# The order of seven products in a two-layer encoder: another tree of sums and bank copies

## Chip, cores and metric

The kernel runs on one core of one Trainium2 chip. The metric is the device time of one execution in microseconds. Before the change three runs gave 909.03, 909.10 and 910.12 us, median 909.1.

## What is computed

The reference is a trunk of two layers on 256 tokens of width 1024, all in float32:

```python
for l in range(DEPTH):   # 2
    x = x + 0.5 * swiglu(rms_norm(x, ffn1_norm[l]), ffn1_w_gate[l], ffn1_w_up[l], ffn1_w_down[l])
    h = rms_norm(x, mix_norm[l])
    ...   # windowed attention and differential attention on h @ w_in[l]
    x = x + jnp.concatenate([out_a, out_b], axis=-1) @ w_out[l]
    x = x + 0.5 * swiglu(rms_norm(x, ffn2_norm[l]), ffn2_w_gate[l], ffn2_w_up[l], ffn2_w_down[l])
return rms_norm(x, final_norm)

def swiglu(h, w_gate, w_up, w_down):
    return (jax.nn.silu(h @ w_gate) * (h @ w_up)) @ w_down
```

The hidden width of an FFN is 2816. The change lies in its products with w_gate and w_up.

## The kernel before

**Products.** A float32 product is made of three matmuls in fp32r: each operand is split into a high part and the rest (low), and high x high, low x high and high x low are added in PSUM. Weights come in blocks of four 128-row chunks by 512 columns (1 MB). SP loads a block into one of six buffers, tile name `raw`. `emit_split` then splits it in two halves: ScalarE casts a half to its high part (`CAST w<-raw`), VectorE subtracts for the low part (`TENSOR_TENSOR w<-raw,w`). A block is multiplied with the 256 tokens; one that meets 128 tokens takes 12 matmuls, one that meets all takes 24.

**Groups by seven.** An FFN's hidden columns are worked in five groups of 512 (0 to 4) and a rest. In 15 groups (2, 3, 4 in the first FFN, 1 to 4 in the other three) gate and up together are a 2 by 2 product: tokens in two halves t, the depth of 1024 in two halves, gate and up as the two columns. The eight products of 12 matmuls are replaced by seven on sums, as in Strassen's scheme. The weight blocks are a (gate, upper depth), b (up, upper), c (up, lower), d (gate, lower). The sums of blocks are made in place: b into a, and c into b, by accumulate DMAs that POOL issues (`gather`; rows `POOL ... DMA raw<-in_ffn_w_up_dram`); c and then d into a by VectorE (`plus`; rows `raw<-raw,raw`). A buffer holds a, then ab, then abc, then abcd, and each is split into w before the next is added. The sums of tokens are made once per FFN by `make_sums` (tiles `q` and `v`).

**Around them.** A group of `by_sevens` also takes two blocks of w_down: dn1 (second column half of the group before last) and dn0 (first half of the group before), 24 matmuls each. dn0 multiplies the hidden block of the group before, which must be transposed first (`turn_one`: four transposes for each of two token halves, a copy `CAST s<-ps` or `s<-xy` to the high part by ScalarE and a subtract by VectorE). The products of a group are summed in PSUM banks `ps` and `xy` with copies by ScalarE. VectorE adds the last sums, ScalarE applies silu, and `up` multiplies into the hidden block (two operations `s<-tmp,hr,tmp`).

**The order.** Every engine works its instructions in the order in which the program issues them (`Kept`). `specs` lists the blocks in the order in which TensorE takes them. `ahead(n)` issues loads, additions and splits for block halves up to number n; where it is called within a group, and how far, stands in the tables `LEAD` (`first` for group 1, `mid`, `last`; other names for the FFN's start and end). A step's `prep` (an addition or an accumulate DMA) is issued once the splits of the step before are.

Of the kernel before, what the change touches and what calls it, by code (L numbers as in the profile page):

```python
# [14 lines left out]
P = 128  # L15
# [15 lines left out]
SEVEN = ((2, 3, 4), (1, 2, 3, 4))  # L31
LEAD = dict(start=(2, 7, 8, 6),
            open0=(2, 0, 0, 2, 3, 6, 8, 6, 5, 6, 1, 10, 1, 5, 7, 6, 8, 0),
            first=(1, 1, 2, 8, 12, 15, 16, 19, 19, 22, 22),
            mid=(2, 8, 12, 12, 15, 15, 20, 20, 20, 22, 23),
            last=(1, 7, 12, 14, 15, 15, 17, 20, 20, 21, 22),
            mid0=(4, 9, 12, 15, 15, 15, 19, 19, 19, 22, 24),
            last0=(2, 8, 12, 13, 15, 15, 19, 20, 20, 22, 25),
            first0=(0, 0, 3, 6, 6, 11, 11, 11, 12, 18, 18),
            open=(10, 11, 9, 7, 11, 11, 9, 5),  # L40
            close0=(6, 3, 7, 5, 6, 10, 3, 10, 5, 11, 4, 6, 1),
            close=(0, 8, 9, 9, 6, 2, 7, 6, 1, 10, 5, 4, 8),
# [4 lines left out]
def trunk(ctx: ExitStack, tc: tile.TileContext, x, n1, g1, u1, d1, nm, w_in, sink,  # L47
# [59 lines left out]
    class Step:  # L107
        def __init__(self, kn, n, moves, key=None, prep=None, src=None, free=None, behind=None, early=0):
            self.kn, self.n, self.moves, self.prep, self.early = kn, n, moves, prep, early
            self.behind, self.added = behind, behind is not None or moves is None  # L110
# [20 lines left out]
    def seven(wg, wu, c0, below, down):  # L131

# [44 lines left out]


# [69 lines left out]
    def ahead(n):  # L248

        n = min(n, 2 * len(specs) - 1)  # L250
        while True:
# [10 lines left out]
            elif at["dma"] < min(at["use"] + AHEAD, len(specs)) and (specs[at["dma"]].moves is None or len(raws) < N_RAW):  # L262
                if specs[at["dma"]].moves is not None:
                    for _ in emit_dma(at["dma"]):
                        pass
                at["dma"] += 1
            else:
                break
# [19 lines left out]
    for l in range(DEPTH):  # L288
        def ffn_specs(wg, wu, wd, sevens):
# [4 lines left out]
            for g in range(1, NGRP):  # L294
                downs = [down(g - 1, h) for h in range(2)]
                if g in sevens:
                    specs.extend(seven(wg[l], wu[l], g * 512, down(g - 2, 1) if g > 1 else None, downs[0]))
# [12 lines left out]
            for n in range(4 if 1 in sevens else 9):  # L310
                specs[base + n].lead = "open" + "0" * (1 not in sevens), n
            for n in range(6):
                specs[n - 6].lead = "close" + "0" * (1 not in sevens), n

        ffn_specs(g1, u1, d1, SEVEN[l > 0])
# [23 lines left out]
        ffn_specs(g2, u2, d2, SEVEN[1])  # L339
# [4 lines left out]
    class Norm:  # L344
# [14 lines left out]
        def turn(self, j, of=range(2), sl=None):  # L359
            sl = halves(bank()) if sl is None else sl  # L360
            for i in of:
                for t in range(2):
                    pe.transpose(sl[:, i, t * P:(t + 1) * P], xk[:, t, (2 * j + i) * P:(2 * j + i + 1) * P], ident)
# [25 lines left out]
        def make_sums(self):  # L389
# [3 lines left out]
            (t0, t1), (b0, b1) = [(t[:, :, 0:P], t[:, :, P:S]) for t in self.xg]  # L393
# [27 lines left out]
            high(s2)  # L421
            yield
            low(2, b0_)
            low(3, s2)
# [262 lines left out]
    def ffn(norm, aside=None, before=None, final=False, sevens=SEVEN[1]):  # L687
# [21 lines left out]
        def prod(xo, w, acc=None):  # L709

            first = acc is None
            if first:
                acc = bank()
# [29 lines left out]
        stage = 0 if before is take_x else 1  # L743

        def by_sevens(h, groups, old):


            flat = lambda: tmp().rearrange("p a n -> p (a n)")
            xy = pair()
            take = lambda: weights(99, True)  # L750
            for g in groups:
                start, late = old is None, g == groups[-1]
                first = 2 * at["use"] - (2 if start else 0)
                caps = iter(LEAD[("first" if start else "last" if late else "mid") + "0" * (stage == 0)])

                def go():
                    ahead(first + next(caps))

                go()
                p1 = prod(norm.quarter(0, 0), take())  # L760
                act.activation(xy[0], p1, AF.Copy, scale=-1.0)
                if start:
                    act.activation(xy[1], p1, AF.Copy, scale=-1.0)
                    new = [turn_one(h, 0)]
                    go()
                    new.append(turn_one(h, 1))
                    go()
                else:
                    below(old, g - 2, 1, take())
                    go()  # L770
                    new = [turn_one(h, 0), turn_one(h, 1, xy[1])]
                    go()
                prod(norm.summed(0), take(), xy[0])
                if not start:
                    act.activation(xy[1], p1, AF.Copy, scale=-1.0)
                go()
                if start:
                    prod(norm.quarter(0, 1), take(), p1)
                below(by_token(new), g - 1, 0, take())
                go()  # L780
                if not start:
                    prod(norm.quarter(0, 1), take(), p1)
                g0 = silu(flat(), p1, 0)
                go()
                old = by_token(new)
                p5 = prod(norm.summed(1), take())
                act.copy(p1, p5)
                go()
                prod(norm.summed(2), take(), xy[1])
                go()  # L790
                prod(norm.summed(3), take(), p5)
                e = flat()
                act.copy(e, p5)
                u1, u0 = flat(), flat()
# [495 lines left out]
```

## Time and profile before

| from the profiled execution | |
| --- | --- |
| median of three runs | 909.1 us |
| span of the profiled execution | 907.5 us |
| TensorE (PE) busy | 899.1 us, 99% |
| VectorE (DVE) busy | 785.9 us, 87% |
| ScalarE (ACT) busy | 609.8 us, 67% |
| GpSimd (POOL) busy | 63.2 us, 7% |
| DMA | 200.83 MB, mean 221 GB/s |

PE is busy in nearly all of the span, and PEld, the weight loads beside the matmuls, in 83% of it. The matmuls are pipelined and their ends modelled, so the starts of the next rows tell more than durations. All busy times are sums over stretches with different limits; the groups by seven are the largest part (twelve of 30.8 us and three first ones of 25.4).

### The profile page before, as it was taken

What the parts mean: (1) busy time and instruction counts of PE and PEld (TensorE: products, weight loads), DVE (VectorE), ACT (ScalarE), POOL (GpSimd) and SP (SyncE); (2) the same over time, 40 slices, a digit from 0 to 9 for tenths busy, and PEclk for the clock granted to TensorE, in tenths of its full rate; (3) what the DMA queues carried; (4) which work ended last, traced back from release to release, by engine and by line L of the source; (5) the groups of instructions that cost most, each with busy time, mean ns of one, the idle gap of its engine ahead of it and who ended that gap; (6) DMA issues with size and microseconds to landing.
All of it is one profiled execution on the core that took longest, in us unless ns stands there. A gap on an engine that the chain in (4) does not pass through costs nothing.

```text
span 907.5 us, 12030 instructions
## 1 busy us (share of the span) xinstructions
PE 899.1 (99%) x4468; PEld 751.0 (83%) x4468; DVE 785.9 (87%) x1069; ACT 609.8 (67%) x970; POOL 63.2 (7%) x79
## 2 busy tenths in 40 slices
PE   9999999999999999999999999999999999999997
PEld 7888888888888888888888888888888888888886
DVE  5968999879987899999778999988888978999894
ACT  6946677666776776677575776667667785776660
POOL 0401000000001001000000001000000000101011
PEclk9999999999999999999999999999999999999999
DMA  9998897954148798897976898899611786898731
GB/s 328 355 287 213 236 309 247 268 143 179 47 150 241 174 265 247 247 300 256 279 204 171 250 278 258 252 303 248 182 57 48 263 223 166 234 312 255 219 114 47
DMA packets 114331, 200.83 MB, mean 221 GB/s; under 512 B 3678, under 2 KB 31648, under 8 KB 114272
## 3 DMA queue, kind: packets, MB, share of 16 engines
q1 hardware_dynamic: 97616, 167.66, 54.4%
q0 software_dynamic: 16096, 31.75, 20.1%
q8 instruction: 35, 0.57, 0.2%
q10 hardware_dynamic: 560, 0.66, 0.2%
q14 instruction: 24, 0.20, 0.1%
HBM read 199.00 MB, written 1.05 MB: 220 GB/s over the span
## 4 chain that ended last, share of the span: by engine, by line
PE 98%; DMA 1%; issue 0%; SPq 0%; DVE 0%; POOLq 0%; POOL 0%
PE ps L62 73%; PE xy L62 25%; DMA xk<-in_x_dram 1%; SPq L172 0%; DVE s L62 0%; DVE xk L62 0%; POOLq L1285 0%; POOL rf L62 0%; SPq L469 0%; SPq L465 0%; DVE tot L62 0%; DVE tmp L62 0%
## 5 line engine op out<-in xcount | busy, mean ns | idle before, releaser
L62 DVE TENSOR_TENSOR w<-raw,w 128x1024 fp32r<-128x1024 f32 (+1 forms) x458 | 476.4, 1097 | 34.6 <-ACT w L62 33.2
L62 PE MATMUL ps<-w,s 128*128 128x512 f32 (+1 forms) x2046 | 473.6, 389 | 0.0
L62 PEld LDWEIGHTS ps<-w,s 128*128 128x128 f32 x2046 | 379.9, 188 | 78.7 <-issue 0.8
L62 ACT CAST w<-raw 128x1024 fp32r<-128x1024 f32 (+1 forms) x457 | 403.9, 954 | 54.0 <-DVE raw L62 38.7
L62 PE MATMUL xy<-w,s 128*128 128x512 f32 x528 | 125.8, 392 | 0.0
L62 PEld LDWEIGHTS xy<-w,s 128*128 128x128 f32 x528 | 98.2, 188 | 20.4
L62 PE MATMUL xy<-w,q 128*128 128x512 f32 x360 | 88.1, 393 | 0.0
L62 PEld LDWEIGHTS xy<-w,q 128*128 128x128 f32 x360 | 66.5, 188 | 13.3
L62 PE MATMUL ps<-s,w 128*128 128x512 f32 (+1 forms) x384 | 69.8, 338 | 0.0
L62 DVE TENSOR_TENSOR raw<-raw,raw 128x2048 f32<-128x2048 f32 x30 | 68.6, 2288 | 0.5
L62 POOL DMA_DIRECT2D raw<-in_ffn_w_up_dram x30 | 38.9, 1313 | 430.1 <-DVE w L62 264.9
L62 PEld LDWEIGHTS ps<-s,w 128*128 128x128 f32 x384 | 58.6, 188 | 8.5
L62 ACT ACTIVATE s<-ps,gcol 128x256 fp32r<-128x256 f32 (+1 forms) x80 | 31.4, 479 | 34.0 <-PE ps L62 34.0
L62 ACT CAST s<-ps 128x512 fp32r<-128x512 f32 x36 | 20.4, 592 | 43.2 <-PE ps L62 43.0
L62 PE MATMUL ps<-w,q 128*128 128x512 f32 x180 | 43.2, 389 | 0.0
L62 PE MATMUL ps<-w,v 128*128 128x512 f32 x180 | 43.2, 389 | 0.0
L62 DVE TENSOR_TENSOR s<-ps,s 128x512 fp32r<-128x512 f32 x36 | 24.1, 686 | 19.5 <-ACT s L62 19.3
L62 PEld LDWEIGHTS ps<-w,v 128*128 128x128 f32 x180 | 33.8, 188 | 7.0
L62 PEld LDWEIGHTS ps<-w,q 128*128 128x128 f32 x180 | 33.8, 188 | 7.0
L62 ACT ACTIVATE s<-s,negm 128x256 f32<-128x256 f32 x64 | 31.8, 498 | 5.3 <-DVE negm L62 5.3
L62 ACT COPY ps<-ps 128x512 f32<-128x512 f32 x15 | 8.6, 570 | 34.4 <-PE ps L62 34.4
L62 DVE SCALAR_TENSOR_TENSOR s<-ps,gcol,s 128x256 fp32r<-128x256 f32 x48 | 20.3, 477 | 13.0 <-ACT s L62 12.9
(131 smaller groups left out, 584.3 us busy)
## 6 DMA issues: line engine op xcount, KB each, us to landing
raw<-in_ffn_w_down_dram SPq DMA_DIRECT2D x44, 1024.0 KB, 7.0
raw<-in_ffn_w_gate_dram SPq DMA_DIRECT2D x39, 1024.0 KB, 7.7
raw<-in_ffn_w_up_dram SPq DMA_DIRECT2D x39, 1024.0 KB, 7.1
raw<-in_ffn_w_up_dram POOLq DMA_DIRECT2D x30, 1024.0 KB, 10.0
raw<-in_w_in_dram SPq DMA_DIRECT2D x14, 1024.0 KB, 6.7
raw<-in_ffn_w_gate_dram SPq DMA_DIRECT2D x8, 512.0 KB, 7.9
raw<-in_ffn_w_up_dram SPq DMA_DIRECT2D x8, 512.0 KB, 8.9
raw<-in_w_in_dram SPq DMA_DIRECT2D x8, 512.0 KB, 6.0
```

Of the source, the lines that this page charges most:

```text
L62: ins = issue(*a, **k)
```

## The change

The seven products are formed by another scheme of sums. In a group TensorE took a, dn1, the transposes, bc, dn0, d, ab, c, abc, abcd (in group 1: a, the transposes, bc, d, dn0, ...). It now takes a, dn1, the transposes, d, dn0, abc, ab, bc, c, abcd (in group 1: a, the transposes, d, dn0, ...). ScalarE made two copies with a factor of -1 (`ACTIVATE xy<-ps`) and two plain ones in a group; now it makes four plain ones (a's bank to Q, abc's to Y, ab's to SBUF, bc's to Q). VectorE added twice and subtracted once from the last product; now it adds twice, and silu of the second half reads the bank itself. The sign goes into `up` by a second scale, minus half of r. `make_sums` makes its four sums in another order. c is loaded beside the step ab; the accumulate DMA to a is issued before the one to b; the tables of how far the splits run ahead are new and stand apart for each FFN. The transposes of the norm have one start and one stop per tile.

```diff
@@ -29,17 +29,28 @@
 N_RAW, N_S4 = 6, 28
 IN_FFN, IN_MIX = 8, 6
 SEVEN = ((2, 3, 4), (1, 2, 3, 4))
+ORDER = (("a", "d", "dn0", "ab", "abc", "bc", "c", "abcd"),
+         ("a", "dn1", "d", "dn0", "ab", "abc", "bc", "c", "abcd"))
...
-            first=(1, 1, 2, 8, 12, 15, 16, 19, 19, 22, 22),
-            mid=(2, 8, 12, 12, 15, 15, 20, 20, 20, 22, 23),
+            next1=(10, 10, 14, 14, 14, 17, 19, 19, 20, 24),
+            more1=(7, 8, 8, 9, 9, 14, 18, 18, 19, 19, 20),
+            last1=(3, 7, 7, 9, 14, 14, 14, 17, 20, 20, 23),
+            open1=(1, 6, 7, 3, 4, 11, 5, 9),
...
-    def seven(wg, wu, c0, below, down):
-
-
-
+    def seven(wg, wu, c0, order):
 
         a, b, c, d = [object() for _ in range(4)]
         w = {a: rows(wg, c0, 512, 0, 4), b: rows(wu, c0, 512, 0, 4), c: rows(wu, c0, 512, 4, 4), d: rows(wg, c0, 512, 4, 4)}
@@ -149,17 +158,23 @@
                 dve.tensor_tensor(raws[to], raws[to], raws[x], op=ALU.add)
             return prep
 
-        steps = [Step(4, 512, load(b), key=b, behind=gather(c, b)), down, Step(4, 512, load(d), key=d, free=[])]
-        if below is not None:
-            steps.insert(0, below)
-        else:
-            steps.insert(1, steps.pop())
-        steps[0].prep = lambda: issue(gather(b, a), 1)
-        return [Step(4, 512, load(a), key=a, free=[])] + steps + [
-                Step(4, 512, None, src=a, free=[]),
-                Step(4, 512, load(c), key=c, free=[]),
-                Step(4, 512, None, prep=plus(c, a), src=a, free=[c], early=1),
-                Step(4, 512, None, prep=plus(d, a), src=a, free=[a, d])]
+        parts = dict(a=Step(4, 512, load(a), key=a, free=[]),
+                     d=Step(4, 512, load(d), key=d, free=[]),
+                     ab=Step(4, 512, None, src=a, free=[], also=(c, w[c])),
+                     abc=Step(4, 512, None, prep=plus(c, a), src=a, free=[]),
+                     bc=Step(4, 512, load(b), key=b, added=True),
+                     c=Step(4, 512, None, src=c, added=False),
+                     abcd=Step(4, 512, None, prep=plus(d, a), src=a, free=[a, d], early=2))
+        steps = [parts[o] if isinstance(o, str) else o for o in order]
+        def begin():
+            if b in raws:
+                issue(gather(c, b), 1)
+            else:
+                parts["bc"].behind = gather(c, b)
+
+        steps[steps.index(parts["a"]) + 1].prep = lambda: issue(gather(b, a), 1)
+        steps[steps.index(parts["d"]) + 1].prep = begin
+        return steps
...
+    def load_also(s):
+        key, src = s.also
+        raws[key] = raw = wp.tile([P, 4, 512], F32, tag="raw", bufs=N_RAW, name=nm_("raw"))
+        sp.dma_start(raw, src)
...
-            def add(x, y, op):
+            def add(x, y):
                 v = tmp().rearrange("p a (c s) -> p (a c) s", c=2)
-                dve.tensor_tensor(v, x, y, op=op)
+                dve.tensor_tensor(v, x, y, op=ALU.subtract)
+                return v
+
+            def less(x, y):
+                v = tmp().rearrange("p a (c s) -> p (a c) s", c=2)
+                dve.scalar_tensor_tensor(v, in0=x, scalar=-1.0, in1=y, op0=ALU.mult, op1=ALU.subtract)
...
-            v = add(t1, t0, ALU.subtract)
-            s1 = add(t1, b1, ALU.subtract)
-            yield
-            high(v)
+            (t0, t1), (b0, b1) = [(t[:, :, 0:P], t[:, :, P:S]) for t in self.xg]
+            s1 = add(b1, t1)
             high(s1)
             yield
-            low(0, v)
-            s2 = add(t0, s1, ALU.subtract)
-            low(1, s1)
-            b0_ = add(b0, s2, ALU.subtract)
-            yield
-            high(b0_)
+            s2 = less(s1, t0)
+            low(0, s1)
             high(s2)
             yield
-            low(2, b0_)
-            low(3, s2)
+            low(1, s2)
+            yield
+            v = add(t0, t1)
+            high(v)
+            yield
+            b0_ = less(s2, b0)
+            low(2, v)
+            high(b0_)
+            yield
+            low(3, b0_)
...
+            self.nhr = tmp("nhr", 2, (P, 2))
+            dve.tensor_scalar_mul(self.nhr, self.r, -0.5)
...
-        def up(h, acc, g, t):
+        def up(h, acc, g, t, by=None):
             n = acc.shape[1]
-            dve.scalar_tensor_tensor(h[:, t, :n], in0=acc, scalar=norm.hr[:, t:t + 1], in1=g, op0=ALU.mult, op1=ALU.mult)
+            by = norm.hr if by is None else by
+            dve.scalar_tensor_tensor(h[:, t, :n], in0=acc, scalar=by[:, t:t + 1], in1=g, op0=ALU.mult, op1=ALU.mult)
...
-        stage = 0 if before is take_x else 1
-
-        def by_sevens(h, groups, old):
-
-
-            flat = lambda: tmp().rearrange("p a n -> p (a n)")
-            xy = pair()
-            take = lambda: weights(99, True)
+        flat = lambda: tmp().rearrange("p a n -> p (a n)")
+
+        def taker(order):
+            left, have = iter(order), {}
+
+            def take(name):
+                while name not in have:
+                    have[next(left)] = weights(99, True)
+                return have.pop(name)
+            return take
+
+        def by_seven(banks, take, go, then):
+
+            A, B, Q, Y = banks
+            prod(norm.quarter(0, 0), take("a"), A, True)
+            act.copy(Q, A)
+            then("a")
+            prod(norm.quarter(0, 1), take("d"), Q)
+            g0 = silu(flat(), Q, 0)
+            go()
+            then("d")
+            prod(norm.summed(1), take("abc"), A)
+            act.copy(Y, A)
+            go()
+            prod(norm.summed(0), take("ab"), B, True)
+            e = flat()
+            act.copy(e, B)
+            go()
+            then("abc")
+            prod(norm.summed(2), take("bc"), A)
+            act.copy(Q, A)
+            u1 = flat()
+            dve.tensor_tensor(u1, A, e, op=ALU.add)
+            go()
+            then("bc")
+            prod(norm.summed(3), take("c"), Y)
+            u0 = flat()
+            dve.tensor_tensor(u0, Y, e, op=ALU.add)
+            h = blk(F32)
+            up(h, u0, g0, 0, norm.nhr)
+            go()
+            prod(norm.quarter(1, 1), take("abcd"), Q)
+            g1 = silu(flat(), Q, 1)
+            go()
+            up(h, u1, g1, 1, norm.nhr)
+            return h
+
+        def by_sevens(h, groups, old, sums):
+
+            A, Q = bank(), bank()
+            B, Y = pair()
+            banks = (A, B, Q, Y) if old is None else (A, Q, B, Y)
+            upto, more = [0], [None]
+
+            def go(table=None):
+                if table is not None:
+                    upto[0] = 2 * at["use"] - (2 if table == "next" else 0)
+                    more[0] = iter(LEAD[table + str(which)])
+                ahead(upto[0] + next(more[0]))
+
             for g in groups:
...
+                go("next" if g == 1 else "last" if g == groups[-1] else "more")
+                new = []
+                take = taker(ORDER[g > 1])
+
+                def then(what):
+                    if what == "a":
+                        if g > 1:
+                            below(old, g - 2, 1, take("dn1"))
+                            go()
+                        for t in range(2):
+                            new.append(turn_one(h, t, banks[1 + 2 * t]))
+                            go()
+                            next(sums, None)
+                    elif what == "d":
+                        below(by_token(new), g - 1, 0, take("dn0"))
+                        for _ in sums:
+                            pass
+                        go()
+
+                h = by_seven(banks, take, go, then)
                 old = by_token(new)
...
+            below(old, groups[-1] - 1, 1, weights(look[0] - 3))
...
```

In the order of the engines, in the second FFN (layer 0), where group 1 begins, ScalarE before: `raw_508` is the buffer of b with c, `raw_509` that of d, `raw_518` that of dn0; `raw_495` is a's. The ACTIVATE rows from `ps_528` are silu, those to `xy` the two copies of product a, the s4 rows the transposed hidden block.

```order
L62 CAST q_562_2925<-tmp_546_2893 128x4x128
L62 CAST q_563_2927<-tmp_547_2895 128x4x128
L62 ACT_TABLE_LOAD
L62 ACTIVATE tmp_567_2961<-ps_528_2793,r_545_2890 128x512
L62 ACTIVATE tmp_568_2963<-ps_529_2794,r_545_2890 128x512
L62 CAST q_569_2965<-tmp_565_2933 128x4x128
L62 CAST v_570_2967<-tmp_564_2930 128x4x128
L62 ACTIVATE xy_572_2998<-ps_575_3003 128x512
L62 ACTIVATE xy_573_2999<-ps_575_3003 128x512
L62 CAST s4_577_3023<-ps_576_3018 128x512
L62 CAST s4_579_3031<-ps_578_3026 128x512
L62 CAST w_582_3084<-raw_495_2610 128x1024
```

Now, with `raw_489` the buffer of a:

```order
L73 CAST w_555_2929<-raw_489_2602 128x1024
L73 CAST w_557_2933<-raw_489_2602 128x1024
L73 ACT_TABLE_LOAD
L73 ACTIVATE tmp_560_2952<-ps_522_2784,r_539_2881 128x512
L73 ACTIVATE tmp_561_2954<-ps_523_2785,r_539_2881 128x512
L73 CAST w_567_2987<-raw_489_2602 128x1024
L73 COPY ps_564_2984<-ps_563_2983 128x512
L73 CAST s4_569_3008<-xy_565_2985 128x512
L73 CAST q_571_3013<-tmp_570_3011 128x4x128
L73 CAST s4_572_3019<-xy_566_2986 128x512
L73 CAST w_573_3022<-raw_489_2602 128x1024
```

The two casts of ab and the first of abc moved from behind the transposed block to ahead of silu, and of the copy to Q. On VectorE at that place, before:

```order
L62 TENSOR_TENSOR w_558_2916<-raw_518_2719,w_557_2915 128x1024
L62 TENSOR_TENSOR w_560_2920<-raw_518_2719,w_559_2919 128x1024
L62 TENSOR_TENSOR q_562_2925<-tmp_546_2893,q_562_2925 128x4x128
L62 TENSOR_TENSOR tmp_564_2930<-s4_542_2865,tmp_547_2895 128x512
L62 TENSOR_TENSOR q_563_2927<-tmp_547_2895,q_563_2927 128x4x128
L62 TENSOR_TENSOR tmp_565_2933<-s4_543_2882,tmp_564_2930 128x512
L62 SCALAR_TENSOR_TENSOR s4_571_2993<-xy_530_2795,hr_548_2897,tmp_567_2961 128x512
L62 SCALAR_TENSOR_TENSOR s4_571_2993<-xy_531_2796,hr_548_2897,tmp_568_2963 128x512
```

And now:

```order
L73 TENSOR_TENSOR w_554_2926<-raw_503_2668,w_553_2925 128x1024
L73 TENSOR_TENSOR w_556_2930<-raw_489_2602,w_555_2929 128x1024
L73 TENSOR_TENSOR w_558_2934<-raw_489_2602,w_557_2933 128x1024
L73 TENSOR_TENSOR raw_489_2602<-raw_489_2602,raw_512_2710 128x2048
L73 SCALAR_TENSOR_TENSOR s4_562_2980<-xy_524_2786,hr_542_2888,tmp_560_2952 128x512
L73 SCALAR_TENSOR_TENSOR s4_562_2980<-xy_525_2787,hr_542_2888,tmp_561_2954 128x512
L73 TENSOR_TENSOR w_568_2988<-raw_489_2602,w_567_2987 128x1024
```

The subtracts of ab and the addition of c moved to ahead of the two operations that make the hidden block (`s4<-xy,hr,tmp`).

The third group of the same FFN, ScalarE around the copies of the transposed block (`s4_686`, `s4_687`), before; `raw_618` is a's buffer:

```order
L62 CAST w_680_3515<-raw_649_3354 128x1024
L62 CAST w_682_3519<-raw_662_3405 128x1024
L62 CAST s4_686_3531<-ps_685_3526 128x512
L62 CAST s4_687_3538<-xy_573_2999 128x512
L62 CAST w_688_3541<-raw_662_3405 128x1024
L62 CAST w_690_3545<-raw_618_3207 128x1024
L62 CAST w_692_3549<-raw_618_3207 128x1024
L62 CAST w_694_3553<-raw_663_3407 128x1024
L62 ACTIVATE xy_573_2999<-ps_677_3473 128x512
```

Now, with `raw_615` as a's buffer and `s4_673`, `s4_674` as the transposed block:

```order
L73 COPY ps_564_2984<-ps_563_2983 128x512
L73 CAST w_671_3505<-raw_615_3207 128x1024
L73 CAST s4_673_3513<-xy_565_2985 128x512
L73 CAST s4_674_3520<-xy_566_2986 128x512
L73 CAST w_675_3523<-raw_615_3207 128x1024
L73 ACTIVATE tmp_677_3540<-ps_564_2984,r_539_2881 128x512
L73 CAST w_678_3566<-raw_615_3207 128x1024
L73 CAST w_680_3570<-raw_615_3207 128x1024
L73 CAST w_682_3574<-raw_649_3372 128x1024
```

The casts of ab stood behind the transposed block; the first now stands ahead of it, and the casts of abc stand just behind, where d's, ab's and c's did.

VectorE at the end of the group ahead of that one, before: the two subtracts of the next a (`raw_618`), then from the last product's neighbours the sums (`tmp`) and the hidden block (`s4_667`):

```order
L62 TENSOR_TENSOR w_657_3393<-raw_618_3207,w_656_3392 128x1024
L62 TENSOR_TENSOR w_659_3397<-raw_618_3207,w_658_3396 128x1024
L62 TENSOR_TENSOR w_661_3402<-raw_630_3267,w_660_3401 128x1024
L62 TENSOR_TENSOR tmp_666_3436<-xy_573_2999,tmp_664_3433 128x512
L62 TENSOR_TENSOR tmp_665_3435<-xy_572_2998,tmp_664_3433 128x512
L62 SCALAR_TENSOR_TENSOR s4_667_3439<-tmp_666_3436,hr_548_2897,tmp_650_3368 128x512
L62 TENSOR_TENSOR tmp_668_3453<-ps_619_3211,tmp_665_3435 128x512
```

And now, with `raw_615` as the next a:

```order
L73 TENSOR_TENSOR w_646_3365<-raw_615_3207,w_645_3364 128x1024
L73 TENSOR_TENSOR tmp_651_3401<-ps_563_2983,tmp_650_3386 128x512
L73 TENSOR_TENSOR w_653_3404<-raw_615_3207,w_652_3403 128x1024
L73 TENSOR_TENSOR tmp_654_3420<-xy_566_2986,tmp_650_3386 128x512
L73 SCALAR_TENSOR_TENSOR s4_655_3422<-tmp_654_3420,nhr_543_2890,tmp_627_3290 128x512
```

The second subtract of a, after which a's accumulate DMA may start, moved to behind the first sum, which waits for product bc.

More of the change, by code (lines that the diff above doesn't have):

```diff
@@ L362, in turn @@
                 for t in range(2):
-                    pe.transpose(sl[:, i, t * P:(t + 1) * P], xk[:, t, (2 * j + i) * P:(2 * j + i + 1) * P], ident)
+                    pe.matmul(sl[:, i, t * P:(t + 1) * P], lhsT=xk[:, t, (2 * j + i) * P:(2 * j + i + 1) * P], rhs=ident,
+                              is_transpose=True, start=i == of[0] and t == 0, stop=i == of[-1] and t == 1)
             return sl
@@ L741, in below @@
             tokens(accs[h], of, w, 4 * g, last=(FC - 1, G4 - 1) if final and h else FC - 1, order=order)
-        stage = 0 if before is take_x else 1
-        def by_sevens(h, groups, old):
-            flat = lambda: tmp().rearrange("p a n -> p (a n)")
-            xy = pair()
-            take = lambda: weights(99, True)
-            for g in groups:
[L752 to L784, printed above, removed]
-                old = by_token(new)
[L786 to L794, printed above, removed]
-                dve.tensor_tensor(u0, xy[1], e, op=ALU.add)
-                dve.tensor_tensor(u1, xy[0], e, op=ALU.add)
-                h = blk(F32)
-                up(h, u0, g0, 0)
-                go()
-                p4 = prod(norm.quarter(1, 1), take(), p1)
-                g1 = flat()
-                dve.tensor_tensor(g1, p4, u1, op=ALU.subtract)
-                go()
-                silu(g1, g1, 1)
-                up(h, u1, g1, 1)
-                go()
-            w = weights(look[0] - 3)
-            below(old, groups[-1] - 1, 1, w)
@@ L870, in ffn @@
             g = gate(gs)
-            next(sums)
         else:
@@ L902, in ffn @@
                 if hh == 0:
-                    next(sums, None)
+                    for _ in sums:
+                        pass
         gu = pair()
@@ L950, in ffn_close @@
         tail(1)
-        ahead(2 * at["use"] + LEAD["close"][-1])
+        ahead(2 * at["use"] + LEAD[f"close{which}"][-1])
         group(1, [(1, t) for t in range(2)])
```

67 lines of the change are left out of this document (37 added, 30 removed).

## Prediction

> **What bounds the kernel now.** I read the page's first part, then the chain.
>
> ```profile
> PE 899.1 (99%) x4468; PEld 751.0 (83%) x4468; DVE 785.9 (87%) x1069; ACT 609.8 (67%) x970; POOL 63.2 (7%) x79
> PE 98%; DMA 1%; issue 0%; SPq 0%; DVE 0%; POOLq 0%; POOL 0%
> ```
>
> TensorE is busy for 899.1 of 907.5 us and carries 98% of the chain: nothing that another engine saves is worth time by itself, since TensorE never waits for it. The profiled span of 907.5 us stands 1.6 us below the median of 909.1 us; I add stalls to the span and then those 1.6 us. About 0.2% (1.8 us) is what a measurement of this kernel can tell from no change.
>
> Then the stretches, one per group of the second FFN (328.01, 358.83) and the third (534.41); columns are PE, PEld, DVE, ACT, POOL, clock, DMA share, GB/s.
>
> ```profile
> 328.01:358.83 30.82, 30.82 (x142) 25.61 (x141) 29.46 (x27) 21.98 (x27) 2.48 (x2) 1.00 0.88 240
> 534.41:565.22 30.81, 30.81 (x141) 25.61 (x141) 29.50 (x28) 21.85 (x27) 2.54 (x3) 1.00 0.92 263
> ```
>
> TensorE fills the whole period at full clock, but VectorE has only 1.3 us to spare and the DMA rings are at 0.9. So the question is whether a reordered group still delivers each operand before TensorE asks. Who asks when, from the PE timeline of one group (start, duration, operation):
>
> ```profile
> 531.75 11.05 PE L62 MATMUL ps<-w,s 128*128 128x512 f32 x48
> 542.64 0.60 PE L62 MATMUL ps<-ident,s 128*128 128x128 f32 x4
> 543.43 2.98 PE L62 MATMUL xy<-w,q 128*128 128x512 f32 x12
> ```
>
> 48 matmuls take 10.89 us, so a product of 12 takes 2.72 and the eight transposes with their switch 0.8 to 0.9. A changed group, from its first matmul: a 0, dn1 2.7, transposes 8.2, d 9.0, dn0 11.8, abc 17.2, ab 19.9, bc 22.6, c 25.4, abcd 28.1, end 30.8.
>
> **The price of the work itself.** Durations by form:
>
> ```profile
> L62 DVE TENSOR_TENSOR w<-raw,w 128x1024 fp32r<-128x1024 f32 x354 | 411.7, 1219 | 30.5 <-ACT w L62 29.3
> L62 ACT CAST w<-raw 128x1024 fp32r<-128x1024 f32 x354 | 348.1, 1051 | 50.9 <-DVE raw L62 38.7 <-DMA raw<-in_ffn_w_up_dram 11.8
> L62 DVE TENSOR_TENSOR raw<-raw,raw 128x2048 f32<-128x2048 f32 x30 | 68.6, 2288 | 0.5
> L62 DVE SCALAR_TENSOR_TENSOR s<-tmp,hr,tmp 128x512 f32<-128x512 f32 x30 | 22.3, 742 | 0.0
> L62 DVE TENSOR_TENSOR tmp<-ps,tmp 128x512 f32<-128x512 f32 x15 | 10.3, 685 | 0.3
> L62 ACT ACTIVATE xy<-ps 128x512 f32<-128x512 f32 x30 | 17.2, 581 | 10.5 <-PE ps L62 10.5
> L62 ACT COPY tmp<-ps 128x512 f32<-128x512 f32 x15 | 8.7, 582 | 5.0 <-PE ps L62 5.0
> L62 ACT COPY ps<-ps 128x512 f32<-128x512 f32 x15 | 8.6, 570 | 34.4 <-PE ps L62 34.4
> L62 ACT CAST s<-ps 128x512 fp32r<-128x512 f32 x36 | 20.4, 592 | 43.2 <-PE ps L62 43.0
> L62 DVE TENSOR_TENSOR s<-ps,s 128x512 fp32r<-128x512 f32 x36 | 24.1, 686 | 19.5 <-ACT s L62 19.3
> ```
>
> The third VectorE operation of a group (685 ns, 15 of them) goes: 10.3 us of VectorE, worth 0, because TensorE covers it. ScalarE still makes four copies per group; 30 negating ones (581) become plain (570 to 582): 0. Four small operations for the second half-scale and eight sums as scalar-tensor-tensor (742 against about 685): 4 x 0.17 + 8 x 0.06 = 1.2 us of VectorE, under TensorE's products outside the groups: 0. TensorE issues the same matmuls: 0. The transposes of the norm with one start and stop per tile: same shapes, 0. The copies that TensorE now needs back: Q after a has the eight transposes as cover in the first group (0.8 against 0.57) and dn1 besides later; Y after abc has ab and bc, 5.4; Q after bc has c, 2.7; with 0.6 each they fit unless ScalarE is held. On the queues: SP loads the same blocks, c with ab rather than ahead of bc; on POOL a's accumulate DMA now precedes b's, and b's waits for its load some 3 us after a's issue, 27 us ahead of the next a's, so it holds nothing. The sum consists only of stalls that the order makes.
>
> **Stall one: the first group of the FFNs two to four.** There a's accumulate DMA and its neighbours run so in the second FFN (POOL's issue, its time to landing from the DMA view of that window, then TensorE and ScalarE):
>
> ```profile
> 290.14 1.31 POOL L62 DMA_DIRECT2D raw<-in_ffn_w_up_dram  x1
> raw<-in_ffn_w_up_dram POOLq DMA_DIRECT2D x1, 1024.0 KB, 8.6
> 298.62 1.28 ACT L62 ACT_TABLE_LOAD   x1
> 302.63 2.88 PE L62 MATMUL ps<-w,s 128*128 128x512 f32 x12
> 305.36 1.04 PE L62 MATMUL ps<-ident,s 128*128 128x128 f32 x8
> 307.48 2.98 ACT L62 CAST w<-raw 128x1024 fp32r<-128x1024 f32 x3
> ```
>
> Before, a+b lands at 298.75 and is first touched at 307.48. Now both casts of a+b, their subtracts and the addition of c stand ahead of the two operations that make the hidden block, which the transposes want at 305.36. The sum: 298.75, two casts (2 x 1.05) to 300.85, second subtract 1.2 to 302.1, addition 2.29 to 304.4, two scalings of 0.7 to 305.1 and 305.8. The second half of the transposes wants it at 305.8, and the cast of abc (waiting for the addition) stands ahead of the copy of Q: 304.4 + 1.05 + 0.57 = 306.0, wanted at 306.2. Slack zero: I take 0.3 each for hand-overs, three times 0.9 us; ends 0 and, with a landing 2 us later, 6.
>
> **Stall two: the later groups.** The tables put a's second half behind the two additions to it, and behind bc's copy. VectorE's subtracts follow each other at 1.15 to 1.2. The hidden block's lows are done 10.6 us into the group (transposes to 9.0, second cast 0.6 to 9.7 at the earliest, its low 0.7, 0.2 of hand-overs); from there the second half of ab 1.15, addition 2.3 and its cast's wait 1.1, abc 2.3, bc 2.3, c 1.15, addition 2.3, c 1.15, abcd 2.3, a 1.15, u1 0.65, a 1.15 = 29.8. So a's accumulate DMA issues 1.0 us ahead of its group, where before it was 1.2 ahead. What differs is who waits: the cast of ab now stands ahead of the casts of the hidden block, and abc at 17.2 is built on it. From landing to the first low half of abc: cast 1.05, ab 1.15, hidden lows 1.2, ab 1.15, addition 2.3, cast 1.1, abc 1.15 = 9.1; TensorE wants that half at 17.6. So the landing may be at 8.5, and the transfer may take 9.4 us. In the first FFN all of a stands ahead of u1, so that by the same sum the issue is 3.5 us ahead of the group; but there ab and the addition stand ahead of the hidden lows, which dn0 wants at 12.0: cast 1.05, ab 2.3, addition 2.3, low 0.7 = 6.3, landing by 5.7, limit 9.2.
>
> What does it take? Before's four, from the DMA view by windows at 326.66, 502.23, 533.18 and 357.63; then the one ahead of the fourth, with its own time, and SP's loads around the third:
>
> ```profile
> raw<-in_ffn_w_up_dram POOLq DMA_DIRECT2D x1, 1024.0 KB, 8.4
> raw<-in_ffn_w_up_dram POOLq DMA_DIRECT2D x1, 1024.0 KB, 8.7
> raw<-in_ffn_w_up_dram POOLq DMA_DIRECT2D x1, 1024.0 KB, 10.7
> raw<-in_ffn_w_up_dram POOLq DMA_DIRECT2D x1, 1024.0 KB, 13.0
> 347.46 1.28 POOL L62 DMA_DIRECT2D raw<-in_ffn_w_up_dram  x1 [19.52 <-DVE w L62]
> raw<-in_ffn_w_up_dram POOLq DMA_DIRECT2D x1, 1024.0 KB, 12.5
> 527.17 0.37 SPq L169 DMA_DIRECT2D raw<-in_ffn_w_gate_dram  x1
> 530.64 0.37 SPq L169 DMA_DIRECT2D raw<-in_ffn_w_up_dram  x1
> 533.18 1.28 POOL L62 DMA_DIRECT2D raw<-in_ffn_w_up_dram  x1 [11.05 <-DVE w L62]
> 537.64 0.37 SPq L169 DMA_DIRECT2D raw<-in_ffn_w_gate_dram  x1
> ```
>
> The first two take 8.4 and 8.7. The third, with loads 6.0 and 2.5 us ahead of it and 4.5 behind, takes 10.7. The fourth's 13.0 has 2.3 us in it for which the one ahead was still moving (347.46 + 12.5 = 359.9). In the change SP's loads follow VectorE's last reads of the buffers: by the sum above bc's end, the second addition, c's end and abcd's end, so 10, 6.5, 5.4 and 3.1 us ahead, and the next 4.5 us behind. Two of these should still move when a's starts, as in the third case, without an accumulate DMA ahead of it: I take 9.8, between the cases and nearer to the third, 0.4 over the limit. The group after it starts from a VectorE some 0.4 later and loses about 0.2. So 0.6 in each of four FFNs, 2.4 us. Ends: 8.4 gives 0; 10.7 gives 1.3 + 1.0 in each, 9.4.
>
> The Trainium skill, "DMA: Bandwidth & Descriptors", section on the anatomy of one SWDGE DMA, fits such a transfer as 2.0 us plus bytes over 436e3 per us. By it 1 MB would land in an estimated 4.4 us, no stall would be left, and the sum would be 909.1; the rows with 8.4 to 13.0 speak against it.
>
> Sum: 907.5 + 0.9 + 2.4 = 910.8 in the span, with the 1.6 outside it **912.4 us**.
>
> **Rivals.** No measurable change (chance 0.36): the accumulate DMAs take 8.4 to 8.7 everywhere, or my chain is 0.5 us too long; then 0 to 1.8 us, about 909.7. For it speaks that the second groups' transfers take that little; against it, that the eight loads of a group stay and that the DMA share of 0.9 leaves little room between them.
>
> The openings are the trouble (0.10): the first transfer is followed directly by the group's second (b's), whose load has long landed. Before, such a pair stands once:
>
> ```profile
> 44.11 2.70 POOL L62 DMA_DIRECT2D raw<-in_ffn_w_up_dram  x2 [5.25 <-DMA raw<-in_ffn_w_up_dram]
> raw<-in_ffn_w_up_dram POOLq DMA_DIRECT2D x1, 1024.0 KB, 13.4
> raw<-in_ffn_w_up_dram POOLq DMA_DIRECT2D x2, 1024.0 KB, 16.6
> ```
>
> The first took 13.4, the pair's median 16.6, so the second 19.8: it ended 7.2 us behind the first. If the pairing cost all of 13.4 - 8.6 = 4.8 us, three openings lose 14.4 on top: 927. If two loads of SP's in flight then did it, as I think, nothing. The skill's same page, section on two DMAs through the same engine, says that descriptors of one queue start in order; the 7.2 us between the pair's ends agree, and by that rule the first loses little.
>
> Faster (0.04): mechanism, TensorE's short gaps at hand-overs close because operands come earlier. Place: all of the span.
>
> ```profile
> 897.78 3.04 PE L62 MATMUL ps<-w,s 128*128 128x256 f32 x24
> ```
>
> The last product ends at 900.82; with 899.1 busy there are 1.7 us not busy up to there, the first load among them. All closed would give 907.4; it decides only from 1.8 us, so the chance is for a matmul pitch that the records don't show to vary.
>
> **Chances.** Forecast, small stalls in several groups, 0.50: 911 to 920. Openings 0.10: 915 to 927. No change 0.36. Faster 0.04. So faster 0.04, same 0.36, slower 0.60. The range for 8 in 10 goes from 908.8 (no stall, run to run) to 919.5: 909.1 + 9.4 + 0.9.
>
> **What would show it.** Right: the groups' period grows from 30.82 to 31 to 32 in the third and fourth group, with TensorE idle ahead of xy or ps<-w,q released by VectorE's w, and ScalarE's casts of w waiting for the POOL DMA; VectorE's busy time falls by about 9 us and saves nothing; TensorE's busy time stays at 899. The first groups' transposes start 0 to 0.5 us late. Wrong: all periods at 30.82 and POOL's median landing at or below 8.7; or gaps of TensorE at the copies of Q and Y, which I costed at 0; or a stall outside the groups, where I found none.

## The result, and the profile after

Four runs of the changed kernel gave 919.77 to 921.69 us, median 921.0; the kernel before ran beside it at 909.17. The ratio is 1.0128 (95% interval 1.0113 to 1.0142): 11.8 us slower, the direction of the forecast, and 1.5 us beyond the upper end of its range. The profiled execution has a span of 918.6 us, 11.1 above that of before.

First the page of the kernel after, the lines that answer to those of before: busy times, granted clock, chain, and the landing of POOL's DMAs. The last line is of after_q_back_256, a run described below in which the matmuls take as long as before.

```profile
PE 908.0 (99%) x4468; PEld 749.6 (82%) x4468; DVE 779.6 (85%) x1058; ACT 610.5 (66%) x970; POOL 61.5 (7%) x79
PEclk9999999999999999999999999999999999999999
PE 92%; DVE 4%; DMA 2%; ACT 1%; issue 1%; SPq 0%; POOLq 0%; POOL 0%; ACTq 0%
raw<-in_ffn_w_up_dram POOLq DMA_DIRECT2D x30, 1024.0 KB, 11.9
PE 906.1 (99%) x4468; PEld 749.8 (82%) x4468; DVE 779.1 (85%) x1058; ACT 610.7 (67%) x970; POOL 61.7 (7%) x79
```

The chain now passes through VectorE, DMA and ScalarE for 7% of the span, as it would where TensorE waits. The first line has the same 4468 matmuls keep TensorE busy for 908.0 us in place of 899.1, at the same clock. That alone doesn't tell slower matmuls from waits: the profile models a matmul of 512 columns as 0.39 us long where the next one starts 0.227 us later, so that short waits count as busy, and 906.1 us remain in the run whose matmuls are as fast as before. The starts have to tell. VectorE gave back 6.3 us, which bought nothing.

The periods of the second and the third group in the second FFN (PE, PEld, DVE, ACT, POOL, clock, DMA share, GB/s):

```profile
329.35:360.51 31.16, 31.16 (x141) 25.63 (x140) 28.59 (x27) 21.11 (x26) 2.57 (x2) 1.00 0.89 245
360.51:391.79 31.28, 31.28 (x142) 25.43 (x141) 28.31 (x26) 21.09 (x27) 2.57 (x2) 1.00 0.92 260
```

They grew from 30.82 to 31.16 and 31.28, also in the second group, for which no wait was forecast. The four products on sums of tokens in group one, from the PE timeline (start, duration, operation), show why:

```profile
318.15 2.96 PE L73 MATMUL ps<-w,q 128*128 128x512 f32 x12
320.95 2.96 PE L73 MATMUL xy<-w,q 128*128 128x512 f32 x12
323.75 2.96 PE L73 MATMUL ps<-w,q 128*128 128x512 f32 x12
326.56 2.96 PE L73 MATMUL xy<-w,v 128*128 128x512 f32 x12
329.35 11.08 PE L73 MATMUL ps<-w,s 128*128 128x512 f32 x48
```

From start to start each product takes 2.80 us, back to back; before, each took 2.72. That is 233.3 ns per matmul, 6.7 more, in all 720 matmuls with q or v: 4.8 us. Products with the tokens' own blocks (s) keep 227. Nothing waits here: the matmuls themselves are slower.

The waits that were forecast are there too. TensorE's weight loads (PEld) waited before:

```profile
PEld ps L62 <- DVE w L62: 0.6, 2, 0.3
PEld ps L62 <- DVE s L62: 0.2, 1, 0.2
```

and after (us in total, times, longest):

```profile
PEld ps L73 <- DVE w L73: 4.2, 12, 0.8
PEld ps L73 <- DVE s L73: 2.8, 5, 1.7
PEld xy L73 <- DVE s L73: 1.1, 5, 0.3
```

These overlap in part with matmuls still running. The largest single one is in the first FFN, in its second group by seven. ScalarE, VectorE and TensorE there, and the time of that group's accumulate DMA to a:

```profile
raw<-in_ffn_w_up_dram POOLq DMA_DIRECT2D x1, 1024.0 KB, 11.3
96.09 2.01 ACT L73 CAST w<-raw 128x1024 fp32r<-128x1024 f32 x2 [3.45 <-DMA raw<-in_ffn_w_up_dram]
97.17 2.36 DVE L73 TENSOR_TENSOR w<-raw,w 128x1024 fp32r<-128x1024 f32 x2 [1.67 <-ACT w L73]
99.57 2.29 DVE L73 TENSOR_TENSOR raw<-raw,raw 128x2048 f32<-128x2048 f32 x1
101.78 0.68 DVE L73 TENSOR_TENSOR s<-ps,s 128x512 fp32r<-128x512 f32 x1
102.51 2.79 PE L73 MATMUL ps<-w,s 128*128 128x512 f32 x11 [1.26 <-DVE s L73]
```

The transfer takes 11.3 us. ScalarE idles 3.45 us until it lands, casts ab, VectorE subtracts and adds c, and only then makes the hidden block's low half, for which TensorE's dn0 has waited. That is the forecast's chain, link by link.

The starts of TensorE's rows share out the loss. From a group's first matmul to the next group's, the 15 groups take 10.2 of the 11.1 us that the span grew by. About 0.35 us in each group, 5.2 in all, is what the groups without a wait lose too: the slower matmuls. The other 5.0 us are waits: 1.5 in the group just shown, 1.0 in the three openings (the first groups of FFNs two to four), 1.0 in their third groups and 1.4 in their fourth. The 0.9 us outside the groups stay open.

### The profile page after: what moved, and what is told of

Read it like the earlier page. It is cut to its first block, busy times and chain, and to the rows that moved or that the text cites. A ratio compares the mean times of both kernels' runs of the same rounds, so it can differ in the third digit from the quotient of the medians.

```text
span 918.6 us, 12062 instructions
## 1 busy us (share of the span) xinstructions
PE 908.0 (99%) x4468; PEld 749.6 (82%) x4468; DVE 779.6 (85%) x1058; ACT 610.5 (66%) x970; POOL 61.5 (7%) x79
## 4 chain that ended last, share of the span: by engine, by line
PE 92%; DVE 4%; DMA 2%; ACT 1%; issue 1%; SPq 0%; POOLq 0%; POOL 0%; ACTq 0%
PE ps L73 66%; PE xy L73 26%; DVE w L73 2%; DVE raw L73 1%; DMA raw<-in_ffn_w_up_dram 1%; ACT w L73 1%; DMA xk<-in_x_dram 1%; DVE s L73 0%; ACT s L73 0%; SPq L187 0%; DVE tmp L73 0%; DVE xk L73 0%; POOLq L1332 0%; POOL rf L73 0%; SPq L501 0%
## 5 line engine op out<-in xcount | busy, mean ns | idle before, releaser
L73 PE MATMUL ps<-w,s 128*128 128x512 f32 (+1 forms) x1974 | 460.3, 390 | 1.3 <-DVE s L73 1.3
L73 PEld LDWEIGHTS ps<-w,s 128*128 128x128 f32 x1974 | 364.7, 188 | 79.4 <-DVE s L73 2.6
L73 PE MATMUL xy<-w,s 128*128 128x512 f32 x600 | 143.8, 392 | 0.0
L73 PE MATMUL ps<-w,q 128*128 128x512 f32 x396 | 97.9, 397 | 0.7 <-DVE w L73 0.4
L73 PEld LDWEIGHTS ps<-w,q 128*128 128x128 f32 x396 | 74.0, 188 | 20.0 <-DVE w L73 2.7
L73 ACT ACTIVATE tmp<-ps,r 128x512 f32<-128x512 f32 x34 | 22.8, 686 | 33.8 <-PE ps L73 33.4
L73 PE MATMUL xy<-w,v 128*128 128x512 f32 x180 | 44.4, 395 | 0.0
L73 PEld LDWEIGHTS xy<-w,v 128*128 128x128 f32 x180 | 33.8, 188 | 8.2
L73 PE MATMUL xy<-w,q 128*128 128x512 f32 x144 | 35.5, 395 | 0.0
L73 PEld LDWEIGHTS xy<-w,q 128*128 128x128 f32 x144 | 27.1, 188 | 6.5
```

What stands on the lines that cost most here:

```text
L73: ins = issue(*a, **k)
```

## Experiments

Two theories had to be told apart for the slower matmuls: the new order of products and banks, or the place of their operands in SBUF. The change has a place in it that the diff hardly shows: `nhr`, two buffers of 8 bytes per partition, placed as 32 each, lies ahead of tmp, q and v in their pool and moves them by 64 bytes. By the addresses of the built programs, in the kernel before q and v begin 160 bytes behind a multiple of 256, and so do all blocks of w and of the tokens; in the kernel after q and v begin at 224.

**The place, in the kernel before.** One number changed, so that unused buffers move q and v, nothing else:

```diff
-            self.hr = tmp("hr", 2, (P, 2))
+            self.hr = tmp("hr", 4, (P, 2))
```

> The kernel before with two more buffers for hr, so that tmp, q and v stand 64 bytes further, as in the kernel after. Theory A (place): its products on q and v go from 226.7 to about 233.5 ns per matmul, 720 x 6.8 ns = 4.9 us, about 914.1 us. Theory B (order or banks): 909.2 us and 226.7 ns.

Measured: 915.18 us, ratio 1.0062 (1.0047 to 1.0077), 5.7 us slower. The products of a group, from the PE timeline:

```profile
558.12 2.96 PE L62 MATMUL ps<-w,q 128*128 128x512 f32 x12
560.92 2.96 PE L62 MATMUL xy<-w,q 128*128 128x512 f32 x12
```

Again 2.80 us: two unused buffers make the kernel before as slow per matmul as the kernel after. The order of products has no part in that. With three and five buffers (32 and 96 bytes):

> The kernel before with one more buffer for hr: q and v 32 bytes further, now a multiple of 64. Theory A says that the place matters but not at which multiple; if the limit is a line of 64 bytes, this place is at least as fast as before's (226.7 ns, 909.2 us); if it is the distance to the blocks of w, which all stand 32 behind a multiple of 64, it is slower. Theory B: 909.2 us.

> The kernel before with three more buffers for hr: q and v 96 bytes further. Theory A: with 64 slow and 128 fast as period, 96 is like one of the neighbours, 909.2 or 914.1 us; the pitch of the products on q and v tells (226.7 or 233.5 ns). Theory B: 909.2 us.

One run each, 914.3 and 914.5 us, with 233 to 234 ns in these products. A multiple of 64 is no cure.

**The place, in the kernel after.** Four buffers for nhr put q and v 128 bytes behind their place before:

```diff
-            self.nhr = tmp("nhr", 2, (P, 2))
+            self.nhr = tmp("nhr", 4, (P, 2))
```

> The kernel after with two more buffers of 8 bytes for nhr (32 bytes each as placed), so that tmp, q and v stand 128 bytes per partition behind their place in the kernel before, not 64. Theory A (place): the products on the sums of tokens (q, v) run at 233.5 ns per matmul because q and v moved by 64 bytes; at 128 they run at 226.7 again as before, 720 matmuls x 6.8 ns = 4.9 us come back, about 916.1 us. Theory B (order or banks): the pitch comes from the new order of the products and their banks; nothing changes, 921.0 us and 233.5 ns.

Measured: 919.9 us, 1.0117 (1.0100 to 1.0134), products at 232.5 ns. The period is not 128 bytes, and theory A in that form was wrong. Eight buffers make it 256:

> The kernel after with six more buffers for nhr, so that q and v stand 256 bytes behind their place in the kernel before: 160 behind a multiple of 256, as before and as all blocks of w. So far 32, 64, 96 and 128 bytes were slow (232 to 234 ns). Theory C (the place within 256 bytes, equal to that of w's blocks, is what counts): the products on q and v return to 226.7 ns, and with what moving by 64 cost the kernel before (913.4 - 907.5 = 5.9 us of the span) the time is about 915.1 us; the rest, some 5 us, are waits. Rival B' (the kernel before's place was fast for another reason, such as its very address): 920 to 921 us.

Measured: 917.4 us, 1.0094 (1.0077 to 1.0111). The products, from the PE timeline:

```profile
314.93 2.88 PE L73 MATMUL ps<-w,q 128*128 128x512 f32 x12
317.65 2.88 PE L73 MATMUL xy<-w,q 128*128 128x512 f32 x12
320.37 2.88 PE L73 MATMUL ps<-w,q 128*128 128x512 f32 x12
323.09 2.88 PE L73 MATMUL xy<-w,v 128*128 128x512 f32 x12
```

2.72 us again, 226.7 ns. The place explains the pitch fully. The time came down by 3.6 us and not by 5.9: the faster products ask earlier, so that some of the gain turned into waits. In the profiled executions the waits within the groups rose from 5.0 to 8.8 us (table below). The 3.6 is rough: the runs of this kernel lie between 916.2 and 922.2 us, and a second measurement of it, further down, gave 919.05. Is it the place itself or the distance between the two operands of a matmul? In the kernel before a constant made 96 bytes longer moves all blocks together:

```diff
-    tables = const.tile([P, 1], F32, name="tables")
-    act.activation(tables, ident[:, 0:1], AF.Silu)
+    tables = const.tile([P, 25], F32, name="tables")
+    act.activation(tables[:, 0:1], ident[:, 0:1], AF.Silu)
```

> The kernel before with a constant tile made 96 bytes longer, so that the blocks of w, the tokens' blocks and q and v all move together to multiples of 256. Theory C in the form that the distance between the two operands of a matmul counts: all products stay at 226.7 ns, 909.4 us. Rival (the absolute place 160 of 256 counts): all 3482 products of 512 columns go to about 233 ns, some 20 us more, about 929 us. If multiples of 256 are better still: below 909 us.

Measured: 909.57 us, ratio 0.9999 (0.9990 to 1.0008), 226.7 ns. So the distance counts, as far as these runs go modulo 256 bytes, and multiples of 256 are no better. before_q_moved_96 agrees: it has q and v at a multiple of 256 and the blocks of w not, and is slow.

**The waits.** What is left, about 8 us over before, was tested from after_q_back_256. First a's accumulate DMA at half its size:

```diff
-                pool.dma_start(raws[to], w[k], accum_op=ALU.add)
+                n = 2 if to is a else 4
+                pool.dma_start(raws[to][:, :n], w[k][:, :n], accum_op=ALU.add)
```

> after_q_back_256 with each group's accumulate DMA to a cut to two of its four row chunks (0.5 in place of 1 MB; the lower chunks of b are left out of ab, abc and abcd). It lands some 3 to 4 us sooner and loads the rings less. Theory (the stalls of the later groups are waits for that landing): the waits of TensorE ahead of dn0, abc and ab go (1.4 us in the first FFN's second group, 0.2 to 0.5 in four others): 2.5 to 3 us below after_q_back_256, about 912.4. Rival (TensorE waits for a VectorE that is late by its own work): no change against after_q_back_256.

Measured: 913.6 us, 1.0044 (1.0031 to 1.0057), 3.8 us less. TensorE waits for a's landing. PEld's waits in after_q_back_256, then here, with the median landing of the halved DMAs:

```profile
PEld ps L73 <- DVE w L73: 5.5, 13, 1.0
PEld ps L73 <- DVE s L73: 3.4, 7, 1.2
PEld ps L73 <- ACT ps L73: 2.0, 4, 0.6
PEld ps L73 <- DVE w L73: 3.1, 10, 0.5
PEld ps L73 <- DVE s L73: 1.7, 6, 0.7
raw<-in_ffn_w_up_dram POOLq DMA_DIRECT2D x15, 512.0 KB, 8.1
```

The halves did not take half the time. In the third and fourth groups of FFNs two to four they took 8.1 to 9.4 us, where whole ones had taken 8.7 to 11.0; they landed 1.5 to 5.0 us sooner in their group mostly because they were issued sooner, 1.9 to 2.4 us ahead of the group in place of 0.2 to 0.6. So an earlier landing also brings the next one forward. The same bytes taken from b's DMA (`n = 2 if to is b else 4`) tell whether the load on the rings was the point:

> after_q_back_256 (917.4 and 919.1 us in two calls) with each group's accumulate DMA to b, not a, cut to half (the lower chunks of c are left out of bc). It is queued directly behind a's and takes 13 to 15.7 us in the kernel after. Theory: b's late landing holds ScalarE at bc's casts and with it the second half of the next a and the copies behind it; without it 2 us or more go, about 915.5. Rival (only a's landing counts, and b's has slack): not below 917.

Measured: 916.97 us, 1.0086 (1.0071 to 1.0100), 0.4 us below the first measurement of after_q_back_256 and 2.1 below the second. It is a's landing above all, and not only the bytes; a share of b's of one or two us is neither confirmed nor excluded. Both at half:

> Both accumulate DMAs cut to half (the lower chunks of b and c left out of the sums). a's half alone gave 913.6 us. If a's half worked by its own landing and b's is a second wait: 912 us or less. If a's half worked by bringing b's landing forward as well, or b's has slack: 913 to 914 us.

Measured: 912.3 us, 1.0032 (1.0019 to 1.0045); the interval meets that of a's half alone, though all six runs (912.3 to 912.5) lie below its four (912.7 to 914.4), so b stays open here too. Then VectorE's additions at half as well as a's DMA:

```diff
-                dve.tensor_tensor(raws[to], raws[to], raws[x], op=ALU.add)
+                dve.tensor_tensor(raws[to][:, :2], raws[to][:, :2], raws[x][:, :2], op=ALU.add)
```

> after_256_half_add with VectorE's additions to a cut to half as well (two of four chunks, 30 x 1.15 us less; the lower chunks of c and d are left out of abc and abcd too). after_256_half_add stands 4.0 us above before. Theory: what is left are VectorE's and ScalarE's chains with no slack (openings, fourth groups); with the additions at half they get 2.3 us per group and about 1.5 to 2 us go, 911.5 to 912 us. Rival: what is left are hand-overs that don't depend on VectorE; 913.6 us.

Measured: 910.8 us, 1.0016 (1.0008 to 1.0025), 2.8 us below a's half alone. VectorE's chain is the second cause. PEld's waits in after_256_half_both, for comparison with the rows above, and the first two products on sums of tokens in the second FFN's fourth group, in after_256_half_add and in after_256_half_both:

```profile
PEld ps L73 <- DVE w L73: 1.5, 7, 0.2
PEld ps L73 <- DVE s L73: 1.2, 6, 0.3
407.65 3.29 PE L73 MATMUL ps<-w,q 128*128 128x512 f32 x12
410.78 1.52 PE L73 MATMUL xy<-w,q 128*128 128x512 f32 x6
407.79 2.88 PE L73 MATMUL ps<-w,q 128*128 128x512 f32 x12
410.51 1.75 PE L73 MATMUL xy<-w,q 128*128 128x512 f32 x7
```

From start to start product abc takes 3.13 us in the first and 2.72 in the second. The starts of all groups show where each cut works: what the groups take beyond those of before, in us, summed by kind, in one profiled execution of each run (for the kernel after less 0.35 per group for the slower matmuls):

| groups by seven | after | after_q_back_256 | after_256_half_add | after_256_half_both |
| --- | --- | --- | --- | --- |
| three of the first FFN | 1.5 | 0.0 | 0.0 | 0.0 |
| openings of FFNs two to four | 1.0 | 1.4 | 0.3 | 0.4 |
| second groups | 0.0 | 0.6 | 0.0 | 0.0 |
| third groups | 1.0 | 4.3 | 1.2 | 0.3 |
| fourth groups | 1.4 | 2.5 | 1.5 | 0.3 |

The openings wait for a's landing, and halving the additions does nothing more for them. The fourth groups lose 0.4 us or more each as long as the additions are whole, also where a lands early: that is VectorE's own chain. In the third groups both count.

Last, a try to mend it: the second half of the next a is split one call of `ahead` earlier, so that its DMA starts sooner.

```diff
-            more1=(7, 8, 8, 9, 9, 14, 18, 18, 19, 19, 20),
+            more1=(7, 8, 8, 9, 9, 14, 18, 19, 19, 19, 20),
```

The same in more2 and more3. A second measurement of after_q_back_256 stands beside it:

> after_q_back_256 once more, as the measure for the other two of this call on the same chip: 915.5 to 918.5 us.

> after_q_back_256 with one number changed in the tables more1 to more3 (18 to 19), so that the second half of the next a is split ahead of u1, which waits for product bc, not behind it; a's accumulate DMA then starts some 0.65 us sooner in the third and fourth groups of three FFNs. Theory (TensorE waits for the landing of a's accumulate DMA): up to six times 0.65 us, where 0.2 to 1.6 are lost now: 1.5 to 3 us below after_256_again. Rival (VectorE is late by its own work): no change.

Measured: 919.05 us (1.0098, 1.0082 to 1.0114) for the measure, a little above its expected span, and 921.85 us (1.0137, 1.0124 to 1.0150) with the earlier split: 2.8 us slower, where 1.5 to 3 faster was expected. PEld's waits, ScalarE and TensorE at the end of a group in after_256_a_earlier:

```profile
PEld ps L73 <- ACT ps L73: 7.3, 6, 1.9
807.85 2.95 ACT L73 CAST w<-raw 128x1024 fp32r<-128x1024 f32 x3 [2.46 <-DVE raw L73]
810.71 0.57 ACT L73 COPY tmp<-xy 128x512 f32<-128x512 f32 x1
811.18 1.04 ACT L73 CAST w<-raw 128x1024 fp32r<-128x1024 f32 x1
812.13 0.58 ACT L73 COPY ps<-ps 128x512 f32<-128x512 f32 x1
812.76 3.49 PE L73 MATMUL ps<-w,s 128*128 128x512 f32 x14 [1.47 <-ACT ps L73]
```

ScalarE had waited 2.46 us for VectorE's addition, so that it came late to ab's copy (810.71), to the cast put ahead (811.18) and to the copy to Q (812.13), which TensorE needs for abcd. The waits for such copies grew to 7.3 us in all, six times, from 2.0 to 2.3, four times, in the two measurements of after_q_back_256; the waits for VectorE fell by less.

## Why the prediction was right and wrong

**The work's price, "TensorE issues the same matmuls: 0".** This step failed. The matmuls are the same in number and shape, but 720 of them take 6.7 ns longer, 4.8 us in all, since the two buffers of a new tile, 64 bytes as placed, moved one operand. "TensorE's busy time stays at 899" was to show the forecast right, and it did not stay. The forecast had a rival in which the pitch varies, on the faster side and at 0.04, and no rival on the slower side. The kernel before with the same shift alone loses 5.7 us. With the operands back in place the kernel after takes 917.4 us, or 919.05 by the second measurement, both inside the range: this step is what took the time out of it. The direction was right without it, because the waits alone make the kernel slower.

**The small operations for the second half-scale at 0.** This was right as work and wrong as a tile: it is the allocation of nhr, not its 0.17 us, that costs.

**Stall two, 2.4 us.** The mechanism held in the third groups and in the first FFN: a's landing, then ScalarE's cast ahead of the hidden block, then the addition, and TensorE's wait at dn0 and abc. a's DMA was issued 0.97 us ahead of the third groups (computed: 1.0) and took 9.1, 9.3 and 9.9 us against the limit of 9.4; 0.1, 0.2 and 0.8 us were lost. In the first FFN's second group by seven it was issued 4.4 us ahead, not 3.5, but took 11.3 where 9.2 was the limit, and 1.5 were lost. Two terms were too small. That transfer was one: 9.8 had been taken for it. The other is the 0.2 for the fourth groups, which lost 0.45 each by VectorE's chain and not as a remainder of the third's. In all 3.9 us in the kernel after, not 2.4. (The terms of the sum that ends at 29.8 add up to 29.6, and four times 2.3 is 9.2, not 9.4; neither decides anything.)

**Stall one, 0.9 us.** This was right, with 1.0 us in the three openings of the kernel after. Part of it shows as "xy <- DVE s", five times, at most 0.3. The slack of zero made it depend on a's landing: with a's DMA at half, 0.3 us are left.

**The sum of the stalls, 3.3 us,** was 5.0 in the groups of the kernel after. With the operands back in place the kernel stands 7.9 us above before (917.4 against 909.5), or 9.6 by the second measurement. Why the third groups lose most there, and differ most from run to run, was not followed up.

**The rival of the openings** (a pair of DMAs slows the first) did not come. The first of the pair in the second FFN, issued at 293.49 with the second 0.9 us behind it, takes, by the DMA view of that window:

```profile
raw<-in_ffn_w_up_dram POOLq DMA_DIRECT2D x1, 1024.0 KB, 8.6
```

As without a follower; in the other two openings it took 8.5 and 8.4. The rule cited from the Trainium skill for it, "DMA: Bandwidth & Descriptors", section on two DMAs through the same engine (descriptors of one queue start in order), agrees.

**The copies of Q and Y at 0** nearly held in the kernel after, where TensorE's weight loads waited 0.4 us for them. The forecast had set the condition "unless ScalarE is held": with the operands back in place they cost 2.0 us, and 7.3 in after_256_a_earlier.

## What to carry to other kernels

A kernel bound by TensorE at 99% can lose only there, and it can lose without a wait: compare the start-to-start time of the same products before and after, not only the gaps. When a change adds or removes any SBUF tile, however small, see where the tiles behind it in the pool come to stand. And a transfer that is moved from long slack to just in time must be priced with its spread, with everything queued behind the first instruction that waits for it.

## What the runs showed of the hardware

In the fp32r products with w as the moving operand (512 columns) and blocks of 128x128 as weights, a matmul takes 226.7 ns where the two operands begin at the same place modulo 256 bytes of a partition, and 232 to 234 ns at a distance of 32, 64, 96 or 128 (q and v moved in either kernel); moving both together changes nothing. Other distances and other types were not run. The 224 products of 512 columns in the attention parts that have w as weights, and alternate with products of 256 columns, take mostly 230 to 241 ns in both kernels, so nothing is shown for them. The Trainium skill, "SBUF — State Buffer", section "Who interferes with whom", gives TensorE two reading ports, one for the moving operand and one for the weights, independent of each other; read as a rule on time, it would have the distance not matter, and the runs show 3%. Whether the ports have to do with it was not found.

An accumulate DMA of 1 MB took 8.3 to 15.7 us in the kernels after, and in the kernel before up to 19.8 (the second of the pair at 44.11). What makes the long ones long, the loads beside them or the one ahead in their queue, was not separated. Those of half the size in after_256_half_add took 5.8 to 10.1.
